# A fused two-block kernel: the state space mixer of its first block rebuilt

## The chip, the cores and the metric

The kernel runs on one core of one Trainium2 chip, as one program. The metric is the device time of that core in microseconds. The engines are TensorE (PE), VectorE (DVE), ScalarE (ACT), GpSimd (POOL) and SyncE (SP); SP issues all DMAs here.

## The reference

Two transformer blocks follow each other on a sequence of 512 tokens of width 1024, in fp32. The change touches the first block only, and in it the state space mixer and the sum of attention weights with values.

```
# first block
h = rms_norm(x, norm_g) * (1 + scale) + shift
ssm_u, ssm_z, q, k, v, attn_z, q_idx, k_idx, w_idx = split(h @ w_in)
y_ssm  = s5_mixer(ssm_u, ...) * silu(ssm_z)          # 32 groups of 16 channels, 64 states each
y_attn = dsa_mixer(q, k, v, q_idx, k_idx, w_idx, ...) * silu(attn_z)   # top 128 keys of each query, 8 heads of 64
x = x + gate * (concat([y_ssm, y_attn]) @ w_out)

# s5_mixer
lam_bar = exp(lam * dt);  b_bar = ((lam_bar - 1) / lam) * b_mat        # complex
bu = einsum('gpc,bsgc->bsgp', b_bar, u)
states[s] = lam_bar * states[s-1] + bu[s]                              # scan over the 512 tokens
y = real(einsum('gcp,bsgp->bsgc', c_mat, states)) + d_skip * u
z = gelu(y);  z = z * sigmoid(z @ w_glu + b_glu)
```

The second block (retention, gated linear attention, sliding-window attention with sinks, a merge of the three and a feed-forward network) follows on the first block's output.

## The kernel before

**How the order of the work is made.** The program is written as plain calls, but nothing is issued at once. Each call goes through a recorder (lines 89 to 198), which notes the engine, the tiles read and written and an estimated duration (`Engine.duration`, line 466). `Recorder.schedule` (line 200) then plays a list scheduler through: each engine takes the ready operation of the lowest key, which is its place in the program less boosts and a multiple of the work behind it. The result is one fixed order per engine; on the chip each engine serves its list strictly in that order. `two` (line 603) offers a two-input operation to DVE and POOL alike if no operand lies in PSUM, `copy` (line 600) offers a copy to ACT and DVE; the scheduler picks. The scheduler also lets no two operations run together that it counts as users of a port shared by DVE and POOL (`Engine.port`, line 456). All DMAs are SP's, in one order.

**Projections.** Weights are loaded as 1 MB units (`wunit`, line 613), and each is split by ACT or DVE into a high part `wh` and a low part `wl` by DVE or POOL, so that a product in the fast fp32r form keeps its accuracy with three products. `proj_a` (line 656) makes token-major results (tokens on partitions), `proj_b` (line 638) feature-major ones.

**The state space mixer.** The 512 tokens are cut into 64 pieces of 8. Within a piece the recurrence is a dense map, between pieces a scan runs over 64 steps. Four batches take 8 groups (128 channels) each.
- `s5_maps(b)` (line 1134) makes, for two sets of 4 groups, the map from 8 tokens of 16 channels to 128 real and imaginary state parts, its transpose `m1`, and the taps of the direct path from input to output within a piece. The tap product is 128 columns wide, of which 16 are kept in four copies a set. The taps go to a scratch tensor `kd`, from which `s5_batch` reads the shifted table `m3` with 8 loads a set.
- `s5_phasors(b)` (line 1164) makes cosine and sine of the turn after 0 to 63 pieces, by six doublings: at level l, six `two` operations on 8 x 2^l columns, from a ladder of squares `wpow`. It adds the decay `mg` of the scan.
- `take_u` (line 1153) writes the mixer's input token-major to a scratch tensor `su`.
- `s5_batch(b)` (line 1190) loads the input in pieces (2 loads), reorders it on ACT, transposes it by 8 products on PE, copies it out of PSUM, multiplies it with `m1` (8 products of 128 columns, half of each kept), turns the result back by the phasors, scans on DVE, turns it forward, and multiplies it with `m2` and `m3`. Turning needs real and imaginary halves swapped (partitions 0 to 63 with 64 to 127): two DMAs before the scan and two behind it. The skip `d_skip * u` is a `two` product and is added as the result leaves PSUM. Gelu follows.

**The attention heads.** `dsa_head(h)` (line 1338) makes logits, exponentials and transposed weights for one of 8 heads, and sums weights with values by 10 products on PE, 128 columns wide (the values of both heads of a pair), of which 64 are kept.

The body (lines 1427 to 1450) records index scores, the projection of the mixer's input, `top_keys` (16 rounds of DVE's max and replace for three blocks of queries), the projections of q, k and v, and then four rounds of `dsa_stacks`, `s5_maps`, `s5_phasors`, `s5_batch` and two heads.

## Time and profile before

| | |
|---|---|
| median of 3 runs | 1555.47 us (1553.98 to 1558.34) |
| profiled execution | 1556.93 us, its span 1555.1 us |
| PE busy | 1465.6 us, 94% of the span |
| DVE busy | 1000.6 us, 64% |
| ACT busy | 434.1 us, 28% |
| POOL busy | 373.2 us, 24% |

The span runs from the first to the last instruction of the profiled execution. Busy time of PE counts a modelled end of each product, so a busy PE may still be served too slowly; each fp32 product shows as two records, an fp32r product or a transpose as one. The helper line 449 stands for every operation, since all go through the recorder, so groups are told apart by tile names: `t` is a working tile in SBUF, `pm` a PSUM bank, `c` a constant tile, `wr`, `wh` and `wl` a raw weight and its parts. In a product's row the moving operand is named first, the stationary one second.

### The profile page before, as it was taken

The numbers are of one execution on the slowest core, as the hardware profiler recorded it, in microseconds if no ns is written. First come the engines' busy times: TensorE is split into PE (matmuls) and PEld (weight loads), VectorE is DVE, ScalarE is ACT, GpSimd is POOL, SyncE is SP. The second block draws the span as 40 slices with busy tenths as digits, with TensorE's granted clock in tenths as the row PEclk, the third lists the DMA queues.
The fourth block names the chain that finished last, engine by engine and source line by source line (L and its number), as shares of the span: only waits on it lengthen the run. The fifth ranks groups of instructions, "written<-read, shape, count | busy, mean of one in ns | idle before, by whom it ended". The sixth has DMA issues, their size and how long they took to land.

```text
span 1555.1 us, 19327 instructions
## 1 busy us (share of the span) xinstructions
PE 1465.6 (94%) x7092; PEld 1210.6 (78%) x7092; DVE 1000.6 (64%) x2098; ACT 434.1 (28%) x911; POOL 373.2 (24%) x465
## 2 busy tenths in 40 slices
PE   6999677877999999999999999999999999999997
PEld 5787466766788888878888888878888888888886
DVE  6997997878874695696435776664467443443434
ACT  4632234443221142252012644431124111110010
POOL 1148694662200123020000232332210111110000
PEclk9999888999999999999999999999999999999999
DMA  9752222444523213312224232212352232332232
GB/s 238 214 177 62 64 55 64 114 119 154 192 78 129 64 55 109 109 33 99 86 81 123 95 102 75 95 49 89 121 203 95 82 108 90 100 122 81 82 135 109
DMA packets 169455, 165.26 MB, mean 106 GB/s; under 512 B 36992, under 2 KB 136200, under 8 KB 169232
## 3 DMA queue, kind: packets, MB, share of 16 engines
q1 hardware_dynamic: 169360, 164.02, 33.9%
q8 instruction: 56, 0.92, 0.2%
q14 instruction: 39, 0.32, 0.1%
HBM read 150.64 MB, written 10.47 MB: 104 GB/s over the span
## 4 chain that ended last, share of the span: by engine, by line
PE 74%; DVE 5%; DMA 1%; ACT 1%; issue 1%; POOL 1%; SPq 0%; DVEq 0%; ACTq 0%; POOLq 0%
PE pm L449 74%; DVE t L449 4%; ACT t L449 1%; DMA t<-t 1%; DVE s L449 1%; POOL t L449 0%; SPq L449 0%; DMA wr<-w_in 0%; DMA wr<-w_out 0%; DVE wl L449 0%; DVE c L449 0%; POOL wl L449 0%; DMA t<-scr_kd 0%; ACT wh L449 0%; DVE wh L449 0%
## 5 line engine op out<-in xcount | busy, mean ns | idle before, releaser
L449 PE MATMUL pm<-c,wh 128*128 128x512 f32 (+1 forms) x1952 | 569.6, 388 | 10.5 <-ACT wh L449 8.0
L449 PEld LDWEIGHTS pm<-c,wh 128*128 128x128 f32 x1952 | 360.1, 189 | 82.3 <-ACT wh L449 9.0
L449 POOL TENSOR_TENSOR t<-t,t 128x512 f32<-128x512 f32 (+11 forms) x267 | 239.0, 910 | 576.2 <-ACT t L449 408.5
L449 PE MATMUL pm<-c,wl 128*128 128x512 f32 (+1 forms) x976 | 327.1, 388 | 11.8 <-DVE wl L449 10.3
L449 DVE CAST wh<-wr 128x1024 fp32r<-128x1024 f32 (+1 forms) x141 | 97.7, 693 | 355.1 <-PE pm L449 347.1
L449 ACT ACTIVATE t<-pm 128x512 f32<-128x512 f32 (+8 forms) x297 | 146.5, 509 | 530.5 <-PE pm L449 499.7
L449 PE MATMUL pm<-t,t 128*128 128x256 f32 (+4 forms) x1232 | 241.6, 326 | 18.1 <-DVE t L449 7.6
L449 DVE TENSOR_TENSOR wl<-wr,wh 128x1024 fp32r<-128x1024 f32 (+2 forms) x186 | 231.4, 1247 | 33.3 <-ACT wh L449 14.7
L449 PEld LDWEIGHTS pm<-t,t 128*128 128x128 f32 (+1 forms) x1232 | 192.1, 192 | 48.7 <-DVE t L449 11.5
L449 PEld LDWEIGHTS pm<-c,wl 128*128 128x128 f32 x976 | 183.2, 189 | 48.7 <-DVE wl L449 11.7
L449 PE MATMUL pm<-wh,c 128*128 128x512 f32 (+1 forms) x576 | 173.1, 385 | 0.0
L449 PE MATMUL pm<-t,wh 128*128 128x512 f32 x416 | 143.4, 396 | 4.7 <-ACT t L449 3.8
L449 PE MATMUL pm<-wh,t 128*128 128x512 f32 x480 | 143.0, 393 | 4.3 <-ACT wh L449 2.7
L449 ACT ACTIVATE t<-t 128x512 fp32r<-128x512 f32 (+6 forms) x149 | 84.4, 577 | 223.7 <-DVE t L449 163.8
L449 POOL TENSOR_TENSOR wl<-wr,wh 128x1024 fp32r<-128x1024 f32 (+2 forms) x26 | 60.6, 2333 | 351.3 <-DVE wh L449 236.3
L449 PE MATMUL pm<-c,t 128*128 128x128 f32 (+4 forms) x638 | 114.5, 299 | 18.7 <-DVE t L449 8.1
L449 ACT ACTIVATE wh<-wr 128x1024 fp32r<-128x1024 f32 (+2 forms) x71 | 73.3, 1034 | 189.7 <-PE pm L449 153.5
L449 PEld LDWEIGHTS pm<-wh,c 128*128 128x128 f32 x576 | 106.8, 189 | 21.2 <-issue 1.3
L449 PEld LDWEIGHTS pm<-c,t 128*128 128x128 f32 (+3 forms) x638 | 81.9, 149 | 42.3 <-ACT t L449 11.2
L449 PEld LDWEIGHTS pm<-wh,t 128*128 128x128 f32 x480 | 90.4, 189 | 24.6 <-issue 3.4
L449 DVE TENSOR_TENSOR t<-t,t 128x512 f32<-128x512 f32 (+11 forms) x157 | 103.4, 673 | 5.4 <-ACT t L449 2.1
L449 PE MATMUL pm<-wl,c 128*128 128x512 f32 (+1 forms) x288 | 102.6, 388 | 2.4 <-DVE wl L449 2.4
(112 smaller groups left out, 1315.1 us busy)
## 6 DMA issues: line engine op xcount, KB each, us to landing
wr<-w_in SPq DMA_DIRECT2D x48, 1024.0 KB, 5.0
wr<-w_branch SPq DMA_DIRECT2D x12, 1024.0 KB, 5.1
wr<-ffn_w_gate SPq DMA_DIRECT2D x11, 1024.0 KB, 5.2
wr<-ffn_w_up SPq DMA_DIRECT2D x11, 1024.0 KB, 5.0
wr<-ffn_w_down SPq DMA_DIRECT2D x10, 1024.0 KB, 5.0
wa<-w_ada SPq DMA_DIRECT2D x32, 256.0 KB, 4.6
wr<-w_out SPq DMA_DIRECT2D x8, 1024.0 KB, 5.0
wr<-w_in SPq DMA_DIRECT2D x12, 512.0 KB, 4.1
```

The source lines that it names most:

```text
L449: self.rec.record(self.eng, lambda: fn(*args, **kw), writes, reads, self.duration(name, writes, reads, kw), self.port(name, writes, reads, ...
```

## The change

- The phasors are made from two tables of 8 (turns by 0 to 7 and by 0, 8, ..., 56 pieces, `phasor_tables`, made once for all groups) by an outer product: six `two` operations of 512 columns a batch. `mg` is a copy on ACT.
- The input projection becomes `proj_b`; `take_u` stores the feature-major result reordered to 8 x 64, and `s5_batch` reads the transposed input by 8 loads a batch. The ordering copies, the transposes and the copy out of PSUM go.
- The tap product has 16 columns, the state product 64; the sum of attention weights with values 64.
- Halves are swapped by a product with a constant matrix `swp`, once before and once behind the scan; the multiplications read the product from PSUM.
- The skip is added to the diagonal of the first tap in `s5_maps`, from a masked table `dskm`; results leave PSUM by copies.
- In the recorder, an fp32 product under 128 columns is priced 125 ns, a DVE operation of one column 150 ns, and a two-input DVE operation on the shared port 0.08 ns a column more.

```diff
--- before.py
+++ after.py
@@ -474,7 +474,7 @@
                 return 109.0 if k > 64 else 68.0
             if reads[0].dtype == F32R:
                 return 9.5 + n * 0.426 if n >= 256 else 219.0
-            return max(219.0, 1.72 * n)
+            return max(219.0, 1.72 * n) if n >= 128 else 125.0
         n = max(n, max((elems(r) for r in reads), default=0))
         points = sum(1 for r in reads[1:] if elems(r) == 1 and n > 8)
         acc = "accum_out" in kw
@@ -491,7 +491,9 @@
             return 80.0 + 2.05 * n
         if name == "tensor_copy" or (name == "tensor_scalar" and not acc):
             return 75.0 + (1.07 if psum else 0.62) * n
-        return 75.0 + 1.045 * n + (62.0 if points else 0.0)
+        if n == 1:
+            return 150.0
+        return 75.0 + 1.045 * n + (62.0 if points else 0.0) + (0.08 * n if self.port(name, writes, reads, kw) else 0.0)
     def transfer(self, dst, src):
@@ -1131,105 +1133,116 @@
     V.memset(zt, 0.0)
     load(kd[128:240, :], zt[:112, :])
+    dskm = t2()
+    load(dskm, bcast_rows(a["d_skip"][0], 512))
+    d3 = dskm.rearrange("p (g c) -> p g c", c=16)
+    two(OP.mult, d3, d3, ident[:, None, 112:128].to_broadcast([128, 32, 16]))
+    swp = const([128, 128])
+    for e in range(2):
+        ACT.activation(swp[:, 64 * e:64 * e + 64], ident[:, 64 - 64 * e:128 - 64 * e], AF.Copy)
     def s5_maps(b):
         kk = t2()
         for q in (2 * b, 2 * b + 1):
             vt = tap_map(q, FR, FI, B0, B1)
             pt, pk = mxp(), mxp()
             for g in range(4):
-                T.matmul(pk[:, g * 128:g * 128 + 128], vt[:, g * 128:g * 128 + 128],
-                         C0[:, b * 128:b * 128 + 128], start=True, stop=True)
+                c = b * 128 + (q % 2) * 64 + g * 16
+                T.matmul(pk[:, g * 16:g * 16 + 16], vt[:, g * 128:g * 128 + 128], C0[:, c:c + 16], start=True, stop=True)
                 T.transpose(pt[:, g * 128:g * 128 + 128], vt[:, g * 128:g * 128 + 128], ident)
-            for g in range(4):
-                c = (q % 2) * 64 + g * 16
-                copy(kk[:, c:c + 16], pk[:, g * 128 + c:g * 128 + c + 16])
+            c = (q % 2) * 64
+            V.tensor_tensor(kk[:, c:c + 64], pk[:, :64], dskm[:, q * 64:q * 64 + 64], op=OP.add)
             m1[q] = t2()
             copy(m1[q], pt)
         load(kd[0:128, b * 128:b * 128 + 128], kk[:, :128])
-    su = dp.tile([512, 512], F32, tag="su", name="scr_su")
-
-    def take_u(ps, t):
+    su = dp.tile([4, 128, 512], F32, tag="su", name="scr_su")
+    def take_u(ps, b):
         ut = t2()
-        copy(ut, ps)
-        load(su[t * 128:t * 128 + 128, :], ut)
+        copy(ut.rearrange("p (t n) -> p t n", t=8), ps.rearrange("p (n t) -> p t n", t=8))
+        load(su[b], ut)
     g3 = lambda ap: ap.rearrange("p (g n) -> p g n", n=64)
     zT = [None] * 4
-    dsk = t2(parts=64)
-    load(dsk, bcast_rows(a["d_skip"][0], 512, parts=64))
     phas = {}
+    def phasor_tables():
+        res = []
+        for lev in (0, 3):
+            r, i = (x.rearrange("p (k g) -> p k g", g=32) for t in (t2(),) for x in (t[:, 0:256], t[:, 256:512]))
+            V.memset(r[:, 0, :], 1.0)
+            V.memset(i[:, 0, :], 0.0)
+            ACT.activation(r[:, 1, :], wpow[lev][0], AF.Copy)
+            ACT.activation(i[0:64, 1, :], wpow[lev][1][0:64], AF.Copy)
+            ACT.activation(i[64:128, 1, :], wpow[lev][1][64:128], AF.Copy, scale=-1.0)
+            for k in (1, 2):
+                if k == 1:
+                    cmul(r[:, 2:3, :], i[:, 2:3, :], r[:, 1:2, :], i[:, 1:2, :], r[:, 1:2, :], i[:, 1:2, :], 1)
+                    cmul(r[:, 3:4, :], i[:, 3:4, :], r[:, 2:3, :], i[:, 2:3, :], r[:, 1:2, :], i[:, 1:2, :], 1)
+                else:
+                    f, fi_ = wpow[lev + 2]
+                    sg4 = pw4[lev // 3]
+                    ACT.activation(sg4[0:64], fi_[0:64], AF.Copy)
+                    ACT.activation(sg4[64:128], fi_[64:128], AF.Copy, scale=-1.0)
+                    cmul(r[:, 4:8, :], i[:, 4:8, :], r[:, 0:4, :], i[:, 0:4, :],
+                         f[:, None, :].to_broadcast([128, 4, 32]), sg4[:, None, :].to_broadcast([128, 4, 32]), 4)
+            res.append((r, i))
+        return res
+    pw4t = t2()
+    pw4 = [pw4t[:, 0:32], pw4t[:, 32:64]]
+    ptab = phasor_tables()
     def s5_phasors(b):
         gs = slice(8 * b, 8 * b + 8)
-        er, ei = t2(), t2()
-        G.memset(g3(er)[:, :, 0], 1.0)
...
+        er, ei, u1, u2 = (t2() for _ in range(4))
+        v4 = lambda ap: ap.rearrange("p (g a c) -> p g a c", g=8, a=8)
+        fine = [x[:, :, gs].rearrange("p k g -> p g k")[:, :, None, :].to_broadcast([128, 8, 8, 8]) for x in ptab[0]]
+        coarse = [x[:, :, gs].rearrange("p k g -> p g k")[:, :, :, None].to_broadcast([128, 8, 8, 8]) for x in ptab[1]]
+        two(OP.mult, v4(u1), coarse[0], fine[0])
+        two(OP.mult, v4(u2), coarse[1], fine[1])
+        two(OP.subtract, er, u1, u2)
+        two(OP.mult, v4(u1), coarse[0], fine[1])
+        two(OP.mult, v4(u2), coarse[1], fine[0])
+        two(OP.add, ei, u1, u2)
+        mg = t2()
+        ACT.activation(g3(mg)[:, :, 1:64], m8g[:, gs][:, :, None].to_broadcast([128, 8, 63]), AF.Copy)
+        V.memset(g3(mg)[:, :, 0], 0.0)
         phas[b] = (er, ei, mg)
     def s5_batch(b):
         er, es, mg = phas[b]
-        ug = []
         uT = t2()
-        pu = mxp()
-        for hq in range(2):
...
+        for t in range(8):
+            load(g3(uT)[16 * t:16 * t + 16],
+                 su[b].rearrange("(g c) (t n) -> t c g n", c=16, t=8)[t])
+        sc_ = t2()
+        pss = mxp()
+        for gg in range(8):
+            T.matmul(pss[:, gg * 64:gg * 64 + 64], m1[2 * b + gg // 4][:, gg % 4 * 128:gg % 4 * 128 + 128],
+                     uT[:, gg * 64:gg * 64 + 64], start=True, stop=True)
+        ACT.activation(sc_, pss, AF.Copy)
+        psw = mxp()
+        T.matmul(psw, swp, sc_, start=True, stop=True)
+        z, sw = t2(), t2()
+        V.tensor_tensor(z, er, pss, op=OP.mult)
+        V.tensor_tensor(sw, es, psw, op=OP.mult)
         two(OP.add, z, z, sw)
         zs, zw = t2(), t2()
         V.tensor_tensor_scan(zs, mg, z, 0.0, op0=OP.mult, op1=OP.add)
-        load(zw[0:64], zs[64:128])
-        load(zw[64:128], zs[0:64])
+        pzw = mxp()
+        T.matmul(pzw, swp, zs, start=True, stop=True)
         xst = t2()
         V.memset(g3(xst)[:, :, 0], 0.0)
+        V.tensor_tensor(zw, es, pzw, op=OP.mult)
         two(OP.mult, zs, er, zs)
-        two(OP.mult, zw, es, zw)
         two(OP.subtract, g3(xst)[:, :, 1:64], g3(zs)[:, :, 0:63], g3(zw)[:, :, 0:63])
         yt = [t2(parts=64), t2(parts=64)]
@@ -1247,14 +1260,10 @@
                 T.matmul(o, xst[:, gi * 64:gi * 64 + 64], m2[:, g * 128:g * 128 + 128], start=True, stop=False)
                 T.matmul(o, uT[:, gi * 64:gi * 64 + 64],
                          m3.rearrange("p (t c) -> p t c", t=8)[:, :, g * 16:g * 16 + 16], start=False, stop=True)
-            du = t2(parts=64)
-            dv = dsk[:, q * 64:q * 64 + 64].rearrange("p (g c) -> p g c", g=4)[:, :, None, :].to_broadcast([64, 4, 8, 16])
             v4 = lambda ap: ap.rearrange("n (g t c) -> n g t c", g=4, t=8)
-            two(OP.mult, v4(du), v4(ug[hq]), dv)
             for th in range(2):
                 yo = yt[th].rearrange("n (t c) -> n t c", t=4)[:, :, hq * 64:hq * 64 + 64]
-                two(OP.add, yo.rearrange("n t (g c) -> n g t c", g=4), v4(py[:64])[:, :, 4 * th:4 * th + 4, :],
-                                v4(du)[:, :, 4 * th:4 * th + 4, :])
+                copy(yo.rearrange("n t (g c) -> n g t c", g=4), v4(py[:64])[:, :, 4 * th:4 * th + 4, :])
         pz = mxp()
         for t in range(8):
             T.transpose(pz[:, t * 64:t * 64 + 64], yt[t // 4][:, (t % 4) * 128:(t % 4) * 128 + 128], ident[:64, :64])
@@ -1371,8 +1380,8 @@
             copy(ptr[:, :w], pt[:, :w])
             def av(i=i, ptr=ptr):
                 for kb in range(i + 1):
-                    T.matmul(po[:, i * 128:i * 128 + 128], ptr[:, kb * 128:kb * 128 + 128],
-                             vt_[kb][:, pr * 128:pr * 128 + 128], start=(kb == 0), stop=(kb == i))
+                    T.matmul(po[:, i * 64:i * 64 + 64], ptr[:, kb * 128:kb * 128 + 128],
+                             vt_[kb][:, h * 64:h * 64 + 64], start=(kb == 0), stop=(kb == i))
             avs.append(av)
             if not AVLATE:
@@ -1382,7 +1391,8 @@
                 av()
         V.reciprocal(ssum, ssum)
         v4 = lambda ap: ap.rearrange("p (t e d) -> p t e d", t=4, e=2)[:, :, e, :]
-        two(OP.mult, v4(osb[pr]), v4(po), ssum[:, :, None].to_broadcast([128, 4, 64]))
+        two(OP.mult, v4(osb[pr]), po[:, :256].rearrange("p (t d) -> p t d", t=4),
+            ssum[:, :, None].to_broadcast([128, 4, 64]))
     zg = {}
@@ -1433,7 +1443,7 @@
     take_ki(pidx[4], 0)
     bias_rows()
     accs = {i: index_scores(i) for i in (1, 2, 3)}
-    proj_a(w_in, 0, 512, hact, take_u)
+    proj_b(w_in, 0, 512, hact, take_u)
     for i in (1, 2, 3):
         selm[i] = top_keys(i, accs[i])
     proj_a(w_in, 1024, 512, hact, take_qk(qn))
```

## Rows read from the trace of the kernel before

**Rows 1.** Stages: stretch, length, busy PE, PEld, DVE, ACT, POOL, clock, DMA

```profile
117.00:178.00 61.00, 57.78 (x281) 47.48 (x279) 51.01 (x144) 17.53 (x33) 44.29 (x90) 0.97 0.20 57
178.00:197.00 19.00, 2.24 (x5) 1.06 (x6) 18.83 (x50) 1.69 (x2) 14.82 (x28) 0.62 0.27 76
197.00:311.00 114.00, 92.64 (x522) 76.72 (x523) 97.91 (x210) 49.65 (x120) 76.31 (x108) 0.88 0.32 79
311.00:428.00 117.00, 96.43 (x505) 77.61 (x504) 96.33 (x160) 41.13 (x89) 45.58 (x33) 0.96 0.50 155
428.00:1556.00 1128.00, 1112.71 (x5324) 925.33 (x5323) 638.87 (x1229) 269.81 (x568) 163.10 (x124) 1.00 0.30 96
```

**Rows 2.** PE's timeline, 177 to 197 us: start, us, what, [idle before, releaser]

```profile
178.69 0.77 PE L449 MATMUL pm<-c,wh 128*128 128x512 f32 x2 [1.48 <-ACT wh L449]
185.25 1.22 PE L449 MATMUL pm<-c,wh 128*128 128x512 f32 x2 [5.79 <-ACT wh L449]
196.74 0.80 PE L449 MATMUL pm<-c,wl 128*128 128x512 f32 x1 [10.27 <-DVE wl L449]
```

**Rows 3.** SP's timeline of DMA issues, 177 to 182 us

```profile
177.72 1.13 SPq L449 DMA_DIRECT2D t<-t  x2
...
180.55 0.38 SPq L449 DMA_DIRECT2D wr<-w_in  x1
```

**Rows 4.** The chain that ended last, 315 to 350 us: start, us, what

```profile
321.14 0.46 SPq L449
...
321.65 2.34 DMA t<-t
...
341.77 0.49 SPq L449
...
342.31 7.34 DMA t<-t
```

**Rows 5.** PE's timeline, fp32 products and transposes, 149 to 334 us

```profile
149.57 1.28 PE L449 MATMUL pm<-t,t 128*128 128x128 f32 x10
150.69 0.38 PE L449 MATMUL pm<-c,t 128*128 128x128 f32 x2
...
151.13 0.27 PE L449 MATMUL pm<-c,t 128*128 128x128 f32 x1
...
332.58 1.28 PE L449 MATMUL pm<-c,t 64*128 64x64 f32 x16 [0.38 <-DVE t L449]
```

**Rows 6.** PE's groups by shape: fp32 products of 512 columns (busy us, mean ns)

```profile
L449 PE MATMUL pm<-t,c 128*128 128x512 f32 x4 | 1.9, 592 | 0.0
```

**Rows 7.** POOL's groups by shape, 0 to 440 us (busy us, mean ns, idle before)

```profile
L449 POOL TENSOR_TENSOR t<-t,t 128x512 f32<-128x512 f32 x48 | 60.9, 1276 | 14.8 <-DVE t L449 7.0 <-issue 4.0 <-DMA t<-t 2.0
...
L449 POOL TENSOR_TENSOR t<-t,t 128x256 f32<-128x256 f32 x13 | 11.7, 906 | 8.2 <-DVE t L449 5.1 <-DVE s L449 1.9 <-PE pm L449 1.1
...
L449 POOL TENSOR_TENSOR t<-t,t 128x32 f32<-128x32 f32 x32 | 11.1, 353 | 3.1 <-DVE t L449 2.7
L449 POOL TENSOR_TENSOR t<-t,t 128x128 f32<-128x128 f32 x20 | 10.4, 528 | 1.0 <-DVE t L449 0.5
...
L449 POOL TENSOR_TENSOR t<-t,t 128x64 f32<-128x64 f32 x23 | 7.8, 347 | 2.8 <-DVE t L449 2.7
L449 POOL TENSOR_TENSOR t<-t,t 128x16 f32<-128x16 f32 x20 | 7.7, 388 | 0.5
L449 POOL TENSOR_TENSOR t<-t,t 128x8 f32<-128x8 f32 x23 | 7.7, 342 | 14.4 <-PE pm L449 12.7 <-DVE t L449 1.4
```

**Rows 8.** DVE's groups by shape, 100 to 430 us

```profile
L449 DVE TENSOR_TENSOR t<-t,t 128x512 f32<-128x512 f32 x43 | 38.1, 898 | 1.1 <-DMA t<-t 0.8 <-ACT t L449 0.2
...
L449 DVE TENSOR_TENSOR t<-pm,t 64x256 f32<-64x256 f32 x16 | 6.0, 410 | 6.9 <-PE pm L449 6.9
...
L449 DVE TENSOR_TENSOR t<-pm,t 128x512 f32<-128x512 f32 x6 | 4.1, 688 | 0.4 <-PE pm L449 0.4
```

**Rows 9.** PE's timeline at the late output products of batch 2

```profile
326.59 5.60 PE L449 MATMUL pm<-t,t 128*64 128x128 f32 x34 [4.88 <-DVE t L449]
```

More of the change, by code (lines that the diff above doesn't have):

```diff
@@ L1183, in s5_phasors @@
-        G.tensor_scalar(ei[64:128], ei[64:128], -1.0, 0.0, op0=OP.mult, op1=OP.add)
-        mg = u1
-        two(OP.mult, g3(mg)[:, :, 1:64], m8g[:, gs][:, :, None].to_broadcast([128, 8, 63]),
-                        ones.rearrange("p (g n) -> p g n", n=64)[:, :, 1:64])
-        G.memset(g3(mg)[:, :, 0], 0.0)
+        er, ei, u1, u2 = (t2() for _ in range(4))
+        v4 = lambda ap: ap.rearrange("p (g a c) -> p g a c", g=8, a=8)
+        fine = [x[:, :, gs].rearrange("p k g -> p g k")[:, :, None, :].to_broadcast([128, 8, 8, 8]) for x in ptab[0]]
@@ L1191, in s5_batch @@
         er, es, mg = phas[b]
-        ug = []
         uT = t2()
-        pu = mxp()
-        for hq in range(2):
-            q = 2 * b + hq
-            uc, uu = t2(parts=64), t2(parts=64)
-            load(uc.rearrange("n (t c) -> n t c", t=8),
-                 su[:, q * 64:q * 64 + 64].rearrange("(n t) c -> n t c", t=8))
-            ACT.activation(uu.rearrange("n (g t c) -> n g t c", g=4, t=8),
-                           uc.rearrange("n (t g c) -> n g t c", g=4, t=8), AF.Copy)
-            ug.append(uu)
-            for g in range(4):
-                T.transpose(pu[:, (4 * hq + g) * 64:(4 * hq + g) * 64 + 64], uu[:, g * 128:g * 128 + 128],
-                            ident[:64, :64])
-        copy(uT, pu)
-        sc_, sw = t2(), t2()
-        for hq in range(2):
-            pss = mxp()
-            for g in range(4):
-                gg = 4 * hq + g
-                T.matmul(pss[:, g * 128:g * 128 + 128], m1[2 * b + hq][:, g * 128:g * 128 + 128],
-                         uT[:, (gg // 2) * 128:(gg // 2) * 128 + 128], start=True, stop=True)
-            for e in range(2):
-                ACT.activation(g3(sc_)[:, 4 * hq + e:4 * hq + 4:2, :],
-                               pss.rearrange("p (g j n) -> p g j n", g=4, j=2)[:, e::2, e, :], AF.Copy)
-        load(sw[0:64], sc_[64:128])
-        load(sw[64:128], sc_[0:64])
-        z = t2()
-        two(OP.mult, z, er, sc_)
-        two(OP.mult, sw, es, sw)
+        for t in range(8):
[12 more added lines that the diff above has]
+        V.tensor_tensor(sw, es, psw, op=OP.mult)
         two(OP.add, z, z, sw)
```

15 lines of the change are left out of this document (removed).

## The prediction

> **What bounds the kernel now.** I read the table by stage first [rows 1]. From 428 us to the end TensorE (PE) is busy 1112.7 of 1128 us at full clock: the second block is bound by PE and nothing in the change touches it. Between 117 and 428 us PE is busy 57.8 + 2.2 + 92.6 + 96.4 = 249 of 311 us, so 62 us are idle, while VectorE (DVE) is busy 264 us and GpSimd (POOL) 181. This stretch holds the state space mixer (S5), the key selection and the attention heads. All that can be won lies here: idle PE time, and PE work that gets shorter.
>
> Then I read who released PE. The worst gap is 178 to 197 us, where PE works 2.2 of 19 us. PE's timeline shows two gaps, 5.8 us for the high part of a weight (ACT) and 10.3 us for its low part (DVE) [rows 2]. The weight was late because SP is one queue in order: two swap transfers (t<-t) that had waited for ACT went out ahead of the load of w_in, which followed at 180.55 [rows 3]. The low part was late because DVE was full (18.8 of 19 us) [rows 1]. The chain of waits then shows the swaps themselves: in batch 2 from 321.14 to 323.99 and in batch 3 from 341.77 to 349.65 nothing on the chain works but SP and the transfer [rows 4].
>
> **The change, part by part.** The sum is made on the profiled execution, 1556.9 us (span 1555.1 and 1.8 around it); the median of the three runs is 1.5 lower.
>
> **Narrow products.** A product of fp32 128x128 by 128 columns shows as two records; five in a row take 150.69 - 149.57 = 1.12 us, 0.224 each [rows 5]. Narrowed are 32 first-tap products (128 to 16 columns), 32 state products (128 to 64) and 80 of attention weights with values (8 heads x 10, 128 to 64): 144. The trace has no narrow fp32 product. From above: 0.224, nothing won, if the two weight loads set the pace. From below: 16 transposes with 64-column inputs take 1.28 us, and a lone one shows 0.27, so (1.28 - 0.27) / 15 = 0.067 a record, 0.133 for two [rows 5]. I take 0.133, as those records also load 128 weight columns: 144 x 0.091 = 13.1 us less (0 to 13.1).
>
> One rule speaks against this: the Trainium skill, "TensorE: Matmul & The Clock Gate", section "LDWEIGHTS (loading the stationary operand)", prices a load by its columns over 1.2 GHz, whatever the rows, which for 128 columns would be an estimate of 107 ns, 213 for two, and the 13.1 us would be 1.5. The row of the 64-row transposes (0.067 with 128 weight columns) contradicts it, though no row has a full 128-row load behind a narrow input.
>
> **Transposes and swaps on PE.** 32 transposes of the mixer's input go: 32 x 0.067 = 2.1 us. Eight swap products 128x128 by 512 columns fp32 come: the nearest row has two such products in four records, 1.9 us, 0.95 each [rows 6], 7.6 us (7.2 at four times the 0.224 of 128 columns). The projection of the mixer's input becomes feature-major: 4 blocks x 8 x 3 = 96 products of 512 columns, as many as the 8 x 4 x 3 before: nothing. PE in sum: -13.1 - 2.1 + 7.6 = -7.6 us (+5.5 without narrowing, -8 at best).
>
> **Phasors.** Before, each of four batches builds its table in six doublings of six products; most of the narrow ones run on POOL. At its prices that is 6 x (0.342 + 0.388 + 0.353 + 0.347 + 0.528 + 0.906) = 17.2 us a batch, 68.7 in all [rows 7]. After: 24 products of 512 columns at 0.898 (DVE) or 1.276 (POOL), 1.09 in the middle, 26 us [rows 7, 8], and once two small tables, 24 operations of 32 columns x 0.353 and 12 of 128 x 0.528, 14.8 us. Saved: 28 us of DVE and POOL. The new views repeat one element or step by 32; no row isolates them. At twice the price the saving would be 2 us; at DVE's 0.688 for operands in PSUM it would be 37.
>
> **Skip and swaps on DVE.** Eight skip products of 512 columns go into the first tap, priced at POOL's 1.276: 10.2 us [rows 7]. The 16 additions behind them (0.410, DVE only) become copies that ACT can also take: about 3.3 of 6.6 us leave DVE [rows 8]. Twelve products (z, sw, zw of four batches) now read PSUM, so DVE alone can do them, 12 x 0.688 = 8.3 us, where before 12 x 1.09 = 13 were shared: 4.7 fewer in sum. The eight ordered copies and a copy of the transposed input leave ACT and DVE, and 32 copies of 16 columns become eight additions; one masked product for the skip, 1.1 us, comes early. In sum some 46 us of DVE and POOL work, chiefly POOL's: 28 + 10.2 + 3.3 + 4.7. DVE itself keeps the key selection and norms and gains the PSUM products, so most of the 46 is off its own list; it gains by POOL standing in its way less (next part) and by handing POOL more.
>
> **What POOL's relief is worth.** DVE's two-input product of 512 columns takes 0.898 with both inputs in SBUF and 0.688 with one in PSUM [rows 8]. The Trainium skill, "SBUF — State Buffer", section "SBUF: two separate sides", says that DVE operations with two SBUF inputs and GpSimd's take turns at one port pair and the loser blocks wholly. The 0.210 between the rows agrees in sign. If it held for all their work, 46 us would come off; but 264 + 181 = 445 us of both ran within 311 us [rows 1], so much of it does overlap.
>
> **Swap transfers on SP.** Sixteen swap transfers go, each at SP's head until DVE or ACT has its data; queued behind them are weight, tap and bias loads. Eight loads of the input per batch (32 KB, plain reads of a scratch tensor written early) replace two: SP issues two more per batch (+6 - 4), some 0.45 each, 3.6 us in all, without a late wait. The waits that a swap now adds sit on PE: behind each swap product stand products of heads and projections; the second needs DVE's scan.
>
> **The path.** Idle PE time that I take back: in 178 to 197 us the 5.8 us behind SP and its 1.5 before it, and 4 of the 10.3 behind DVE: 11. In batch 2, 2.85 us of SP and transfer become a product of 0.95: 2. In batch 3, 7.9 us become about 1.2; as PE has other work in part of it, 5 of 6.7. In 197 to 311 us (21.4 idle) a share of POOL's relief: 5. Together 23 of the 62. What is late next is the selection's chain on DVE and the heads. A higher clock in 178 to 311 us, 0.62 and 0.88 now, of levels 1.2 and 2.4 GHz, would come on top [rows 1]; I count none. Sum: 1556.9 - 23 - 7.6 = 1526.3; less 1.5 for the median: about 1525.
>
> **Planner.** Its prices change for narrow products, for one-column and for two-SBUF-input operations, so the order moves everywhere. In the second block PE has only 15.3 us idle [rows 1]; reordering can cost or give a few us, zero in the middle.
>
> **Rivals.**
> A, DVE keeps the clock: selection, norms and weight splits fill DVE, the PSUM products bind it further, and narrow products stay at 0.224. Then PE loses 2.1 and gains 7.6, and of the idle time only SP's part and the two swaps return (7.3 + 2 + 5 = 14): 1556.9 + 5.5 - 14 - 1.5 = 1547. For it: DVE at 99% where PE is idle longest. Against: the 0.067.
>
> B, slower: PE stops behind the swap products. Each of eight waits in order for DVE or ACT with its PSUM data; where a swap transfer blocked SP alone, now PE stands. If each stops PE by the 4.9 us that batch 2 shows for one late S5 product [rows 9], that is 39 us, against 23 + 7.6 = 31 won: 1556.9 + 8 - 1.5 = 1563. It decides from 3.8 us a swap. For it: DVE serves in order and is nearly full. Against: the planner puts other products ahead of one whose input is late, and the chain before had the same scan with a transfer more.
>
> C, DVE and POOL fully take turns, and PE waits for that: all 46 us of their work come off, with PE's 7.6: 1556.9 - 53.6 - 1.5 = 1502. For it: 0.898 against 0.688; against: the 445 in 311 us. (The Trainium skill's port rule above would make it so.)
>
> **How the numbers follow.** Forecast 0.55 (own range 1510 to 1542), A 0.20, B 0.15, C 0.10. A change under 0.3%, 4.7 us, can't be told from none: faster is below 1550.8, slower above 1560.1. The forecast and C are faster, A in 0.16 of its 0.20, B slower in 0.12 and the same in 0.03: 0.81, 0.07, 0.12. The range 1502 to 1556 leaves out half of C and most of B, 0.18.
>
> **What would show it.** Right: no t<-t transfer on SP but key copies; attention products of 64 columns at 0.13 to 0.15; phasor products of 512 columns in place of the small ones on POOL; the gap at 178 to 197 us half as long; POOL's time before 428 us lower by 30 or more; the block's end, where PE becomes full, at about 398 us in place of 428. Wrong: PE waits on DVE behind swap products; 64-column products at 0.22; new phasor products at 1.8 or more; DVE still full where PE is idle, with the gap as before.

## The result, and the profile after

The changed kernel is slower: 1569.01 us (median of 8 runs, 1561.30 to 1571.96) against 1555.28 us of the kernel before beside it (8 runs, 1552.17 to 1558.50), a ratio of 1.0072 with an interval of 1.0048 to 1.0096 (ratios are taken over all runs, so they are not exactly the quotients of the medians). Five of the eight runs took 1569.0 to 1572.0 us, the profiled one among them, and three 1561.3 to 1562.1. I had forecast 1525. The profiled span grew from 1555.1 to 1567.3 us.

The table by stage, as [rows 1], of the kernel after (stretch, length, busy PE, PEld, DVE, ACT, POOL, clock, DMA):

```profile
117.00:178.00 61.00, 58.98 (x289) 48.82 (x288) 48.32 (x136) 16.93 (x27) 47.10 (x69) 1.00 0.17 51
178.00:197.00 19.00, 16.34 (x64) 12.76 (x64) 15.89 (x33) 4.16 (x7) 12.53 (x19) 0.82 0.31 84
197.00:311.00 114.00, 69.91 (x335) 55.07 (x334) 81.63 (x211) 32.23 (x67) 35.21 (x43) 0.67 0.19 50
311.00:428.00 117.00, 103.88 (x579) 84.20 (x578) 94.38 (x165) 51.49 (x116) 56.72 (x42) 0.97 0.52 161
428.00:1567.00 1139.00, 1124.49 (x5378) 936.16 (x5376) 655.14 (x1242) 268.07 (x573) 161.55 (x126) 1.00 0.30 96
```

Three things are to be read here beside [rows 1].
- The gap at 178 to 197 us is nearly gone: PE is busy 16.34 of 19 us where it was 2.24.
- A new one opens behind it: from 197 to 311 us PE falls from 92.64 to 69.91 us and the granted clock from 0.88 to 0.67. From 117 to 428 us PE's busy time sums to 249.1 us in both kernels, so exactly as much is idle (61.9 us).
- What differs is the clock at which it is busy: 0.91 before and 0.86 after in the mean of 117 to 428 us. Busy time times granted clock, a rough measure of work done, gives by stage 56.0 + 1.4 + 81.5 + 92.6 = 231.5 us before and 59.0 + 13.4 + 46.8 + 100.8 = 220.0 us after. The 11.5 us that are missing at 428 us are nearly the 12.2 us of the span. In the last stage PE is idle 14.5 us, before 15.3: the second block only starts later.

PE's timeline of the changed kernel in the new hole (start, us, what, [idle before, releaser]):

```profile
206.72 1.11 PE L449 MATMUL pm<-c,t 128*128 128x128 f32 x4 [8.51 <-DVE t L449]
...
228.24 0.48 PE L449 MATMUL pm<-c,t 128*128 128x128 f32 x1 [3.43 <-DVE t L449]
...
246.90 0.80 PE L449 MATMUL pm<-t,t 128*128 128x256 f32 x2 [11.95 <-DVE t L449]
249.49 2.07 PE L449 MATMUL pm<-t,c 128*128 128x512 f32 x2 [1.79 <-DVE t L449]
```

The table by stage of the middle of it:

```profile
225.00:250.00 25.00, 4.25 (x11) 2.69 (x12) 21.57 (x43) 3.45 (x7) 0.00 (x0) 0.50 0.09 21
```

PE waits for DVE, the longest time 11.95 us, and works 4.25 of 25 us while DVE is busy 21.57 and POOL not at all. DVE's timeline just before that shows with what:

```profile
232.94 0.19 DVE L449 TENSOR_TENSOR t<-t 128x32 f32<-128x32 f32 x1
...
237.39 8.76 DVE L449 TENSOR_TENSOR t<-t,t 128x512 f32<-128x512 f32 x10
246.16 1.28 DVE L449 TENSOR_TENSOR t<-t,pm 128x512 f32<-128x512 f32 x2
...
248.21 1.22 DVE L449 TENSOR_TENSOR_SCAN t<-t,t 128x512 f32<-128x512 f32 x1
```

And POOL's, at the same time:

```profile
217.94 0.25 POOL L449 TENSOR_TENSOR t<-t 128x32 f32<-128x32 f32 x1
252.46 1.29 POOL L449 TENSOR_TENSOR t<-t,t 128x384 f32<-128x384 f32 x1 [34.27 <-DVE t L449]
```

The last small operation on POOL, of 32 columns, ends at 218 us and the second phasor table on DVE at 237 us. Ten of the twelve wide operations that make the phasors of two batches then stand in DVE's list, 8.76 us, ahead of the two multiplications that read the state product out of PSUM (246.16). The first of these needs the phasors, and its end releases PE at 246.90, by the shape (128x256) for a product of an attention head. Why a head waits for that operation the trace does not say. The state product of that batch and its swap were made at 176.63 and 179.29, and these two PSUM banks of the program's eight stayed taken until then; that PE lacked one of them is likely, but not shown. POOL, which could do the wide operations, has been idle for 34 us. The new mixer did take work off both engines: from 117 to 428 us DVE and POOL are busy 240.2 + 151.6 = 391.8 us, where it was 445. But it left the rest in an order that PE waits for. (Part of the 53 us has only moved behind 428 us: over the whole run the two are busy 989.1 + 343.6 us in place of 1000.6 + 373.2, 41 us less.)

### The profile page after: what moved, and what is told of

Its sections match the earlier page's. It is cut to its first block, busy times and chain, and to the rows that moved or that the text cites. A ratio compares the mean times of both kernels' runs of the same rounds, so it can differ in the third digit from the quotient of the medians.

```text
span 1567.3 us, 19147 instructions
## 1 busy us (share of the span) xinstructions
PE 1475.9 (94%) x7076; PEld 1217.8 (78%) x7076; DVE 989.1 (63%) x2084; ACT 423.9 (27%) x889; POOL 343.6 (22%) x366
## 4 chain that ended last, share of the span: by engine, by line
PE 86%; DVE 7%; DMA 3%; SPq 2%; issue 1%; ACT 1%; POOL 0%; DVEq 0%; ACTq 0%; POOLq 0%
PE pm L449 86%; DVE t L449 5%; SPq L449 2%; DVE s L449 1%; ACT t L449 1%; DVE wl L449 1%; DMA t<-x 0%; DMA wr<-w_out 0%; DMA wr<-w_in 0%; POOL wl L449 0%; DMA wr<-w_glu 0%; DMA wr<-w_ada 0%; DMA t<-t 0%; DMA t<-log_dt 0%; DMA wa<-w_ada 0%
## 5 line engine op out<-in xcount | busy, mean ns | idle before, releaser
L449 PE MATMUL pm<-c,wh 128*128 128x512 f32 (+1 forms) x2016 | 593.4, 390 | 3.3 <-ACT c L449 2.0
L449 DVE CAST wh<-wr 128x1024 fp32r<-128x1024 f32 (+2 forms) x154 | 107.1, 696 | 348.7 <-PE pm L449 347.1
L449 ACT ACTIVATE t<-pm 128x512 f32<-128x512 f32 (+9 forms) x286 | 151.1, 544 | 521.7 <-PE pm L449 510.4
L449 POOL TENSOR_TENSOR t<-t,t 128x512 f32<-128x512 f32 (+9 forms) x153 | 174.2, 1151 | 487.2 <-ACT t L449 294.5
L449 PE MATMUL pm<-t,t 128*128 128x256 f32 (+6 forms) x1232 | 243.4, 325 | 26.6 <-DVE t L449 19.3
L449 POOL TENSOR_TENSOR wl<-wr,wh 128x1024 fp32r<-128x1024 f32 (+2 forms) x32 | 76.2, 2382 | 354.9 <-DVE wh L449 284.1
L449 PE MATMUL pm<-wh,c 128*128 128x512 f32 (+1 forms) x512 | 150.8, 381 | 1.4 <-DVE wh L449 1.4
L449 ACT ACTIVATE t<-t 128x512 fp32r<-128x512 f32 (+7 forms) x143 | 78.0, 556 | 235.2 <-DVE t L449 190.5
L449 DVE TENSOR_TENSOR t<-t,t 128x512 f32<-128x512 f32 (+8 forms) x139 | 115.9, 844 | 13.1 <-ACT t L449 8.5
L449 DVE TENSOR_TENSOR t<-pm,t 128x512 fp32r<-128x512 f32 (+9 forms) x149 | 81.2, 554 | 37.7 <-ACT t L449 20.7
```

Source lines behind the costliest of these rows:

```text
L449: self.rec.record(self.eng, lambda: fn(*args, **kw), writes, reads, self.duration(name, writes, reads, kw), self.port(name, writes, reads, ...
```

## The experiments

Two theories. P: the time is made by the order that the list scheduler draws, which any new price or new operation draws again; "order" is meant to hold the choice of engine too, where the scheduler has one. M: the new operations are bad in themselves, the late outer product on DVE above all.

**Prices.** The changed kernel with the two DVE prices of before; the old operations with the two new ones; and the changed kernel without the port price alone.

```diff
-        if n == 1:
-            return 150.0
-        return 75.0 + 1.045 * n + (62.0 if points else 0.0) + (0.08 * n if self.port(name, writes, reads, kw) else 0.0)
+        return 75.0 + 1.045 * n + (62.0 if points else 0.0)
```

> The changed kernel with the recorder's two old prices for DVE operations (one-column operations and two-input operations on the shared port); the mixer's arithmetic is the changed one. Theory P (the loss is the order that the recorder makes with its new DVE prices: the phasor tables come late on DVE and PE stands at 200 to 260 us): 1525 to 1545, the hole shorter by half. Theory M (the loss is the new mixer itself: all phasors wait for the whole ladder of squares, swap products stop PE): 1560 to 1572, the hole stays.

> The kernel before with only the two new DVE prices of the recorder, every operation as before. Theory P: slower than before by 15 to 40 us (1570 to 1595). Theory M: 1550 to 1560, as before.

> The changed kernel without one of its two new VectorE prices, the 0.08 ns a column for instructions that read or write by the port that VectorE and GpSimd share; the other (150 ns for one column, and the lower base) stays. If the port's price, which makes VectorE look dearer where both engines could take a wide product, is what sends work the wrong way: 1545 to 1553, as with both old prices. If it is the other price, or the order alone: 1558 to 1572.

Measured: 1546.33 us (ratio to before 0.9920, 0.9894 to 0.9946); 1569.37 (1.0070, 1.0048 to 1.0091); 1549.06 (0.9943, 0.9922 to 0.9964). No operation differs between the first, the third and the changed kernel, and 20 us come and go. Together with the kernel before and the changed one this makes a square at one constant: the two new prices cost 14 us with the old operations (1555 to 1569) and 23 with the new (1546 to 1569); the new operations gain 9 us under the old prices and nothing under the new (1569.37 against 1569.01). The first two times lie within 1.5 us of theory P's ranges. But P had also asked of the first run that the hole shrink by half, and it did not. The 12 us wait stands in the faster orders too, with 11.35 us in the first run; here it is in the run without the port price:

```profile
244.63 1.01 PE L449 MATMUL pm<-t,t 128*128 128x384 f32 x2 [11.33 <-DVE t L449]
```

So that wait belongs to the new operations, and it is not what parts a good order from a bad one. Ten-microsecond stretches show one place where the two part. First the changed kernel, then the one without the port price:

```profile
260.00:270.00 10.00, 5.39 (x26) 3.76 (x24) 4.75 (x8) 4.24 (x9) 2.07 (x2) 0.67 0.13 29
270.00:280.00 10.00, 8.73 (x37) 6.72 (x37) 7.17 (x17) 4.15 (x10) 3.65 (x4) 0.67 0.30 77
280.00:290.00 10.00, 10.00 (x57) 8.71 (x57) 5.34 (x12) 5.04 (x12) 3.82 (x5) 0.83 0.57 145
```

```profile
260.00:270.00 10.00, 8.74 (x61) 7.26 (x60) 9.83 (x22) 7.06 (x18) 9.01 (x7) 1.00 0.48 126
270.00:280.00 10.00, 10.00 (x68) 8.67 (x68) 7.41 (x21) 6.65 (x16) 4.83 (x4) 1.00 0.63 171
280.00:290.00 10.00, 10.00 (x75) 8.94 (x73) 7.70 (x11) 4.06 (x8) 8.38 (x5) 1.00 0.21 45
```

After the same hole one order has all four engines at work at once, and the clock is back to its upper level (2.4 GHz) from 260 us on; the other feeds PE thinly, and its mean of 0.67 to 0.83 says that a part of each stretch is still at the lower level (1.2 GHz).

**Narrow products alone, with the order redrawn and with the order held.** The old kernel, the 80 products of attention weights and values narrowed; in the first run with the new price of 125 ns, in the second with the price kept at that of 128 columns, so that every engine's list is the one of before: the trace has the same sequence of instructions on PE, DVE, ACT and POOL.

```diff
-            return max(219.0, 1.72 * n)
+            return max(219.0, 1.72 * n) if n >= 128 else 125.0    # first run
+            return max(219.0, 1.72 * max(n, 128))                  # second run
```

> The kernel before with only the 80 products of attention weights and values narrowed to 64 columns (and their price). If a narrow fp32 product costs 0.133 us: PE's busy time falls by some 7 us, the time by 3 to 8 if the order holds; if weight loads set the pace at 0.22 each, no change of PE's time. In both theories the order may move by some us either way.

> The kernel before with one edit: the 80 attention value products are 64 columns wide instead of 128, and the price that the list scheduler puts on them is held at that of 128 columns, so that the order of the work on every engine stays the one of the kernel before. Of the prediction's step on narrow products: a narrow product takes 0.133 us against 0.224 us, so 80 of them give back up to 80 x 0.091 = 7.3 us, and the time is 1548 to 1555. The rival (the two weight loads of an fp32 product set its time, since the changed kernel's trace has a 64-column record at 0.113 us, 0.227 us a product): no gain, 1554 to 1557. Either way it has to stay far below the 1580 us of the same edit under its own price, if that time was the order's.

Measured: 1579.63 us (1.0128, 1.0087 to 1.0169) and 1556.41 (1.0004, 0.9985 to 1.0023). This pair separates best: the same operations, and 23 us by the scheduler's choices alone (the redrawn run has 454 instructions on POOL where the held one has 465, so a few changed engine). Held in order, narrowing is worth nothing that can be seen (2 us of gain to 4 of loss); the 7.3 us that the prediction had for these 80 products are excluded. The stages from 197 us, first of the redrawn order, then of the held one:

```profile
197.00:311.00 114.00, 85.29 (x450) 71.11 (x450) 86.84 (x197) 44.40 (x107) 66.49 (x108) 0.75 0.23 59
311.00:428.00 117.00, 84.75 (x449) 69.58 (x449) 85.75 (x158) 37.19 (x82) 44.79 (x36) 0.84 0.42 130
```

```profile
197.00:311.00 114.00, 94.02 (x534) 77.92 (x533) 97.91 (x212) 50.85 (x122) 77.79 (x109) 0.89 0.33 84
311.00:428.00 117.00, 96.65 (x493) 77.78 (x492) 94.09 (x159) 39.59 (x87) 42.34 (x33) 0.93 0.47 152
```

The held one repeats [rows 1]; the redrawn one loses busy time and clock in both.

**The outer product.** Its tables moved ahead in the scheduler's order, in the changed kernel; and, in exactly the changed kernel's order, four of its six products a batch cut short.

```diff
+    rec.boost = S5BOOST
     ptab = phasor_tables()
+    rec.boost = 0
```

```diff
+    cut = lambda *x: tuple(y[:, :1] for y in x)
...
-        two(OP.mult, v4(u1), coarse[0], fine[0])
+        two_(OP.mult, v4(u1), coarse[0], fine[0], cut(v4(u1), coarse[0], fine[0]))
...
-        two(OP.subtract, er, u1, u2)
+        two_(OP.subtract, er, u1, u2, (v4(er), coarse[0], fine[0]))
```

> The changed kernel with the phasor tables recorded at the boost that the ladder of squares has, so that they are ready sooner. If the late tables make the hole at 200 to 260 us (a part of M, and of P): 1535 to 1555. If something else does, such as the rest of DVE's order: 1560 to 1575.

> The changed kernel in exactly its own order, with the four products of each batch's phasors (16 instructions of 512 columns, 0.88 us each on VectorE) cut to 64 columns and the two sums reading the tables instead of the products; the phasors are then wrong numbers, everything else is computed. If the hole at 200 to 250 us is made by these products, which stand on VectorE ahead of the first heads, it closes by up to 4 to 6 us and the time is 1560 to 1565. Rival (VectorE is only full there because the table behind the ladder of squares comes late, or the heads' own work fills it): the products' time is covered and it stays within 3 us of the changed kernel's 1569.

Measured: 1551.35 us (0.9953, 0.9931 to 0.9974) and 1560.31 (1.0006, 0.9981 to 1.0032). The first is also a redraw, under the new prices, and its time does not speak for late tables: the second table is ready only 3 us sooner (234 us) and the wait is nearly as long, so most of the 18 us came from elsewhere in the order.

```profile
244.06 1.01 PE L449 MATMUL pm<-t,t 128*128 128x384 f32 x2 [11.33 <-DVE t L449]
```

In the second, the row of DVE's ten operations and that of PE's wait read

```profile
239.93 4.99 DVE L450 TENSOR_TENSOR t<-t,t 128x64 f32<-128x64 f32 x10
```

```profile
245.70 0.80 PE L450 MATMUL pm<-t,t 128*128 128x256 f32 x2 [6.65 <-DVE t L450]
```

4.99 us on DVE where the changed kernel has 8.76 (the row names the first shape only: six cut products and four sums), and 6.65 us of waiting where it has 11.95. With two cut products ahead of the ten, 0.65 us in place of 2.21, DVE has 5.33 us less to do and PE waits 5.30 us less, in the same sequence of instructions on PE, DVE, ACT and POOL: what these operations cost DVE is in the path in full, and a part of M is true. The median falls by 8.7 us, the profiled span by 2.7 only, because PE enters the hole 4 us later in this trace than in the other. It is not the whole: the hole keeps its other waits.

This run also prices the views. In the changed kernel a product that reads the tables through repeated and strided views takes 1.03 to 1.06 us on DVE, and a sum of the same 512 columns of plain tiles 0.68 to 0.69, POOL idle at both. The first two rows show one of each; in the third, of the run with cut products, such a sum reads the tables' views instead:

```profile
238.37 1.03 DVE L449 TENSOR_TENSOR t<-t,t 128x512 f32<-128x512 f32 x1
```

```profile
239.32 0.68 DVE L449 TENSOR_TENSOR t<-t,t 128x512 f32<-128x512 f32 x1
```

```profile
240.29 1.05 DVE L450 TENSOR_TENSOR t<-t,t 128x512 f32<-128x512 f32 x1
```

All four sums take 1.04 to 1.05 us there. So the views cost half as much again, 0.36 us an operation, and the run undersells what the cut products took: it made the sums dearer.

**The order redrawn.** One constant of the scheduler moved, `TAIL` in line 38, the weight of the work behind an operation; no operation changes.

```diff
-TAIL = 12.0
+TAIL = 11.5
```

With the old operations:

> The kernel before with its operations untouched and one constant of the list scheduler moved (TAIL, the weight of the work that hangs behind an operation, 11.5 instead of 12), so that only the order is drawn again. Theory P (the kernel before stands on an order that happens to be good for its own prices, and any edit that draws the order again loses 10 to 25 us of it): 1562 to 1580. Rival (the order is robust and the new prices or the new mixer are bad in themselves): 1552 to 1560.

> The kernel before with TAIL at 12.1 instead of 12, the smallest step tried. If its order at 12 is a draw that only stands there (theory P): 1565 to 1580, as its redraws at 11.5 and 13.0. If a small step keeps it: 1553 to 1560. Against 1541 of the changed operations with old prices at the same constant, the new operations would then be worth 12 to 39 us.

> The kernel before with its operations untouched and TAIL at 13.0 instead of 12: a second redraw of its order, on the other side of its value. If the kernel before stands on an order better than its neighbours (theory P): 1565 to 1585, as the redraw at 11.5 (1580). If the redraw at 11.5 was an unlucky one and most orders are as good as the kernel before's: 1550 to 1562.

With the new operations and the old DVE prices:

> The changed kernel with the old VectorE prices and TAIL at 11.5, where the kernel before gave 1580. If the new operations are worth 10 us or more at equal constants: 1545 to 1568. If not: 1570 to 1585.

> The changed kernel with the two old VectorE prices and TAIL at 12.1, a third redraw, and a candidate for a version that beats both kernels: 1538 to 1552 if a small step of the constant keeps what made the run at 12.0 good; 1555 to 1578 if each draw stands for itself.

> The changed kernel with the two old VectorE prices (as the run of 1546 us) and the constant TAIL moved to 12.5, so that its order is drawn once more. If the new mixer is worth something beside its order, it stays below the redrawn kernel before by more than 10 us: 1545 to 1556. If the 1546 us were a lucky draw of their own and the mixer is worth nothing: 1560 to 1575, as high as the redrawn kernel before.

> The changed kernel with the two old VectorE prices and TAIL at 13.0: its second redraw. If the new operations are worth 10 us beside their order: 1550 to 1565, under the redraws of the kernel before; if they are worth nothing: 1565 to 1585, as those.

With the new operations and the new prices:

> The changed kernel as it is, new VectorE prices too, with TAIL at 12.1. If the new prices are bad in themselves, it stays 10 us or more above the same kernel with old prices at this constant (1541): 1555 to 1580. If 1569 was only the draw at 12: 1538 to 1555.

> The changed kernel with its new prices and TAIL at 13.0; with old prices this constant gave 1560, the kernel before 1573. Prices bad in themselves: 1568 to 1585. Prices neutral, the draw alone: anywhere in 1540 to 1575, so that the mean over three constants with new prices is within 8 us of that with old.

Medians in us (ratio to before and its interval):

| TAIL | old operations, old prices | new operations, old DVE prices | new operations, new prices |
|---|---|---|---|
| 11.5 | 1580.46 (1.0118 to 1.0172) | 1561.99 (1.0009 to 1.0039) | |
| 12.0 | 1555.28, the kernel before | 1546.33 (0.9894 to 0.9946) | 1569.01 (1.0048 to 1.0096), the changed kernel |
| 12.1 | 1593.05 (1.0183 to 1.0236) | 1541.36 (0.9875 to 0.9909) | 1565.76 (1.0026 to 1.0064) |
| 12.5 | | 1576.56 (1.0065 to 1.0126) | |
| 13.0 | 1573.04 (1.0072 to 1.0116) | 1559.95 (1.0007 to 1.0035) | 1569.88 (1.0050 to 1.0101) |

The ratios are to the runs of the kernel before beside each run, whose medians lie 1 to 3 us above 1555.28; the differences below are of the medians shown.

The kernel before stands on an order better than all that its neighbours give: the smallest step loses 38 us, and the draws at 11.5 and 13.0 lose 25 and 18. At each of the four constants that both have, the new operations with the old prices are faster than the old ones, by 18.5, 9, 52 and 13 us. The run at 12.5 has no partner, and by itself, at 1577, it lies where I had said that the mixer is worth nothing. The new prices are slower than the old in all four pairs that differ in nothing else, by 23, 24 and 10 us with the new operations and by 14 with the old. The test set for the last run, that neutral prices bring the means over three constants within 8 us, failed: 1568 against 1549. So the rival that these prices are bad in themselves stands, and the runs lean its way; against it speaks only that a change of constant moves the time by as much, up to 38 us, and that 1569 is better than three of the four old-price draws of the old operations.

The stages of the two runs at 12.1, old operations first:

```profile
117.00:178.00 61.00, 46.63 (x218) 38.81 (x219) 52.33 (x131) 17.44 (x39) 45.83 (x70) 0.85 0.18 56
178.00:197.00 19.00, 19.00 (x92) 15.26 (x91) 18.90 (x50) 4.23 (x9) 14.91 (x28) 0.95 0.28 71
197.00:311.00 114.00, 65.03 (x354) 53.46 (x353) 79.64 (x211) 32.49 (x70) 33.64 (x71) 0.75 0.22 59
311.00:428.00 117.00, 84.64 (x503) 70.05 (x502) 86.94 (x173) 39.47 (x98) 45.28 (x53) 0.87 0.38 115
```

```profile
117.00:178.00 61.00, 58.98 (x297) 49.57 (x296) 47.33 (x133) 17.55 (x27) 48.10 (x61) 1.00 0.19 55
178.00:197.00 19.00, 15.78 (x70) 12.10 (x68) 15.87 (x40) 5.35 (x10) 11.53 (x20) 0.91 0.27 74
197.00:311.00 114.00, 77.75 (x441) 62.13 (x442) 99.77 (x236) 45.35 (x97) 51.17 (x60) 0.78 0.29 74
311.00:428.00 117.00, 110.50 (x580) 90.41 (x578) 94.28 (x178) 47.85 (x102) 39.70 (x28) 0.96 0.49 160
```

Busy time times clock from 117 to 428 us is 180 us in the first, 240 in the second, and their spans are 1592.4 and 1537.5: 60 us of work missing, 55 us of time. The kernel before has 231.5 and the one after 220.0. The old operations at 12.1 have no gap at 178 to 197 us, the very one that I had set out to win back, and are the slowest of all.

**The swaps.** The new operations with the old DVE prices, halves swapped again by two DMAs, at two constants.

```diff
...
-        pzw = mxp()
-        T.matmul(pzw, swp, zs, start=True, stop=True)
+        load(zw[0:64], zs[64:128])
+        load(zw[64:128], zs[0:64])
...
-        V.tensor_tensor(zw, es, pzw, op=OP.mult)
+        two(OP.mult, zw, es, zw)
```

> The changed kernel with the old VectorE prices (1546 us), its halves swapped again by two DMAs each, as before the change, instead of a product. The prediction's step: 8 swap products cost TensorE 7.6 us and take away DMA latencies of 2.3 us and more, for a gain of a few us after all. If the products are the better way: 1549 to 1565. If TensorE's 7.6 us are simply lost (rival B: it stops behind them): 1536 to 1545. The order is drawn again, so that only both constants together speak.

> The same at TAIL 12.1, where the swaps by products gave 1541. Products better: 1545 to 1565; their TensorE time lost: 1530 to 1540.

Measured: 1564.91 us (1.0058, 1.0039 to 1.0077) and 1565.50 (1.0038, 1.0017 to 1.0059), 19 and 24 us above the same with products. Both are also new draws, and not only the swap differs: the first two multiplications read SBUF and may go to POOL again. So the size is uncertain; the sign is the same twice, which is a hint and no more where draws move by as much.

The version at 12.1 with the old DVE prices beats both kernels: 1541.36 us, 0.9892 of before (0.9875 to 0.9909). It too has the wait in the hole; what could be won there was not tried:

```profile
239.25 0.79 PE L449 MATMUL pm<-t,t 128*128 128x256 f32 x2 [11.39 <-DVE t L449]
```

Two runs are missing: the new operations with the price of narrow products held, and the old doublings beside the other new operations. The first would tell how much of the loss that third price makes; with the old operations its redraw cost 23 us.

## Why the prediction was wrong, step by step

**The step that failed is "Planner": "reordering can cost or give a few us, zero in the middle".** I looked for its effect in the second block, where PE has little idle time, and found none there; that part held (14.5 us idle against 15.3). It acts in the first block. There the two new DVE prices alone cost 14 us with the old operations and 23 with the new, the price of narrow products 23 us (values narrowed, held against redrawn), and a constant of the scheduler alone up to 38 us (`TAIL` 12 against 12.1). And zero is not its middle. Six orders of the old operations (1555, 1569, 1573, 1580, 1580, 1593) have a mean of 1575: the kernel before lies 20 below it. Ten orders of the new operations, leaving out the cut products and the swaps by DMA, have a mean of 1559: the kernel after lies 10 above it. The means differ by 16 in favour of the new operations. That 20 + 10 - 16 = 14 is the measured loss is arithmetic and proves nothing. If the draws stand for all orders, the new operations are worth about 16 us, half of what I forecast, and the change gave back more by leaving a good draw for a poorer one. But that is an estimate: six and ten draws that scatter by 12 to 13 us leave the 16 uncertain by some 6, and at the constant of the two kernels, under the prices of the changed one, the gain was 0.4 us. What is shown is that the planner's new order cost 14 to 23 us where the prediction had put zero; why these prices lead to poorer orders stays open.

**The path: "together 23 of the 62" idle us: none came back in sum.** The first 11, in 178 to 197 us, did, and 3 more: 14.1. In 311 to 428 us, where the swaps of batches 2 and 3 had been given 7, idle time fell by 7.5. But from 197 to 311 us, where I had counted on 5 more, 22.7 us were added: PE ran out of that work sooner and stood instead. I had asked what is late next and named "the selection's chain on DVE and the heads", and priced it at nothing. **The clock**, which I left out as a gain, became the loss: from 225 to 250 us it is 0.50, the lower level (1.2 GHz). It had fallen when PE had stood for 8.5 us before 206.72, and PE stood for another 12 us at 234.9.

**Narrow products: 13.1 us, measured nothing but 0.9.** Their records after, on PE's timeline of the changed kernel (16 columns, then 64):

```profile
167.75 0.96 PE L449 MATMUL pm<-t,t 128*128 128x16 f32 x8
...
176.63 1.97 PE L449 MATMUL pm<-t,t 128*128 128x64 f32 x16 [0.23 <-issue]
179.29 1.13 PE L449 MATMUL pm<-t,c 128*128 128x512 f32 x2 [0.69 <-ACT t L449]
180.23 0.73 PE L449 MATMUL pm<-c,wh 128*128 128x512 f32 x2
```

Less the 0.27 of a lone record, 1.97 us is (1.97 - 0.27) / 15 = 0.113 a record, 0.227 a product; 16 columns give (0.96 - 0.27) / 7 = 0.099, 0.197 a product, which for 32 of them is 0.9 us less; 128 columns were at 0.224 [rows 5]. Even the 0.9 is an upper value, since start to start the records of 16, 64 and 128 columns all follow each other after 0.112 us at the upper clock. The upper bound held and the value I took was wrong, because its row was of the wrong kind: transposes load 64 rows, these products 128. The Trainium skill, "TensorE: Matmul & The Clock Gate", section "LDWEIGHTS (loading the stationary operand)", which I set aside for that row, gives an estimate of 107 ns for 128 weight columns; the records agree with it within 6% at the upper clock. (At the lower one, 16 records of 64 columns took 3.65 us at 219.48, nearly twice as long.) Its remark that the rows do not matter is what the 0.067 of 64 rows speaks against.

**Swap products: right in price.** 180.23 - 179.29 = 0.94 us each at full clock against 0.95 (2.07 at half clock in the hole). Rival B, PE stopping behind them, had the nearest time (1563) and is refuted as a mechanism: the 20 records of that form after, ten products with the eight swaps among them, have 6.7 us of idle time before them together, 3.1 of it before the swaps, where B wanted 39. A kin of it is true: PE waits 11.95 us for the multiplication that reads these products out of PSUM, in faster and slower orders alike, and no part of my sum had that. The row of the 20 records:

```profile
L449 PE MATMUL pm<-t,c 128*128 128x512 f32 x20 | 12.6, 723 | 6.7 <-DVE t L449 5.3 <-ACT t L449 0.7 <-DVE s L449 0.7
```

**DVE and POOL work: right in sum.** 46 us fewer forecast; 41 measured over the whole run, and 445 - 391.8 = 53 in the same stretch. The phasor operations cost 8.76 / 10 = 0.876 us in the mean, between the 0.688 and the 1.09 that I had used, but that mean hides two prices: six products with the views at 1.03 to 1.06 and four plain operations at 0.68 to 0.69. POOL's price held, 1287 ns against 1276, and so did that of a product with an operand in PSUM, 684 ns against 0.688:

```profile
L449 POOL TENSOR_TENSOR t<-t,t 128x512 f32<-128x512 f32 x55 | 70.0, 1287 | 38.0 <-PE pm L449 21.1 <-DVE t L449 15.4 <-issue 0.7
```

```profile
L449 DVE TENSOR_TENSOR t<-t,pm 128x512 f32<-128x512 f32 x14 | 9.5, 684 | 9.5 <-PE pm L449 7.8 <-ACT t L449 1.6
```

The comparison of 0.898 with 0.688, which I took for a sign of the shared port, was a mean of the same kind. Of the 43 operations behind the 0.898 [rows 8], the 20 that ran while POOL was idle took 0.66 to 0.69 us, as those with an operand in PSUM do; of the 23 that ran beside POOL, ten took 0.66 to 0.70 and thirteen 0.89 to 2.12. So two inputs in SBUF cost nothing by themselves, and what is lost is lost beside POOL, some of the time.

What I missed is when that work comes: by the program the doublings could begin at the first square, while the outer product needs the ladder and a table first. It made less work and later work, and the 34 us that POOL waits before 252 us are a sign of it.

**Rival A** had PE's side right (narrow at 0.224), and the runs at 1546 to 1551 lie on its 1547 by chance: it too priced the order at nothing. **Rival C** falls: 41 us came off DVE and POOL over the run, and none of it off the time.

What stays open: which pair of operations in the list makes one draw good and the next bad. The wait of 11.3 to 12.0 us behind DVE's first multiplication stands in seven orders of the new operations whose times run from 1541 to 1570 us; in others the holes lie elsewhere (17.2 us before 212 in one with DMA swaps, 18.5 us before 342 in the redrawn narrow one). So no single wait explains the difference.

## What to carry to other kernels

Where the order of a kernel comes out of a planner, an edit is two changes: its own and a new order. Hold the order (keep the old price beside the new instruction) to measure the first, and move a constant that changes no operation to see the size of the second, before the edit is judged or its gain forecast. Set edits and prices in a square, each with and without the other, before one of them is blamed. Ask of a rebuilt chain not only what it costs but what must be done before its first operation; no run here isolates what the later start was worth, but shortening the outer product took its full time off PE's wait. And take an operation's price from a row of the same kind in all its sizes, the stationary operand's rows too, and look behind a mean before two means are compared.

## What the runs showed of the hardware that was not expected

- An fp32 product of 16, 64 or 128 columns with a 128-row stationary operand took nearly the same time, 0.20 to 0.23 us, while transposes with a 64-row operand ran at 0.067 a record [rows 5].
- A DVE product of 512 columns that read its inputs through repeated and strided views took 1.03 to 1.06 us, a plain sum or product 0.66 to 0.69 with POOL idle, whether or not an operand lay in PSUM; beside POOL the plain ones took up to 2.12.
- The same idle time cost different amounts: kernels with the same 249.1 us of busy PE from 117 to 428 us did 231.5 and 220.0 us of work by busy time times clock. In the slower one most idle time lay from 197 to 311 us (44 us idle, clock 0.67), in the other it was spread further (21 there, clock 0.88).
